# Splitting the last selection group into two pairs and giving score tiles a third PSUM buffer

## Chip, cores and metric

One core of one Trainium2 chip. The metric is the device time of one execution in microseconds (us); several runs are taken and the median is given. TensorE (PE), VectorE (DVE), ScalarE (ACT), GpSimd (POOL) and SyncE (SP, which only issues DMAs here) each work through their own list of instructions in order; semaphores tie the lists together. PSUM, into which TensorE writes, has 8 banks of 512 float32 values for each of 128 partitions, and both kernels use all eight in the stage that is changed.

## What is computed

One layer of a hybrid decoder: a combined projection of x (4096 positions, 1024 features) feeds a sparse attention branch and a state-space branch (S5); both are gated, joined, projected and normalised. The sparse attention first gives every query a score for every earlier key, and keeps the best 256 keys (n_sel is 256, the heads of the scores are 8 of 32):

```python
idx_logits = jnp.einsum('bthd,bsd->bths', qi_b, ki)
index_score = jnp.einsum('bths,bth->bts', jax.nn.relu(idx_logits), wi_b)
index_score = jnp.where(causal[None], index_score, neg)
_, sel = lax.top_k(index_score, n_sel)
c_sel = jax.vmap(lambda cb, ib: cb[ib])(c, sel)
s = jnp.einsum('bthc,btkc->bthk', ql_b, c_sel)
s = jnp.where(valid[:, :, None, :], s, neg)
p = jax.nn.softmax(s, axis=-1)
o = jnp.einsum('bthk,btkc->bthc', p, c_sel)
...
mixed = jnp.concatenate([att * jax.nn.silu(gate_a), ssm * jax.nn.silu(gate_s)], axis=-1)
y = jnp.einsum('bse,ed->bsd', mixed, w_out)
return layer_norm(DEEPNORM_ALPHA * x + y, ln_g, ln_b)
```

All results are float32. The products that need it are made from a high and a low part of each operand in three matmuls (a triple, `mm3`, lines 98 to 100).

## The kernel before

The 4096 positions are 32 tiles of 128 queries. The kernel runs in three stretches: scores, selection and projection together (to about 1790 us), attention with the S5 branch woven into it (to about 3500 us), and the output (to the end).

**The first stretch** has two streams. The projection goes over the positions in eight sweeps of 512 (`prepare` transposes x with TensorE, L483; `sweep` takes 17 columns of the weights and multiplies, 24 matmuls to a column, L98 to L100 on tiles `ps_x`). ScalarE and VectorE empty `ps_x`, and SyncE stores the results. From the second sweep on, POOL loads the split weights from memory (L511), two tiles `w` to a column. The column "kv" makes the keys and values of attention from the latents `c_d` (L513 to L535): eight triples, each emptied by ScalarE (L85) and VectorE (L87) into tiles `st`, of which there are three, and stored to `k_d` (16 stores) and `v_d` (8 stores). The column "ckv" makes the latents, with small sums on TensorE at L574 and L582.

The other stream makes the scores of a query tile (`score`, L238 to L266): TensorE multiplies into `ps_i` (L254, two banks to a tile), ScalarE takes relu of it (L256), VectorE adds it with the head's weight to the row of scores `acc` (L265). Then `select` (L296 to L406) finds the 256th largest score of each row for a group of tiles at a time. It works in up to 8 rounds: count how many scores are above a threshold, move the threshold. The count of one tile goes to VectorE (L329) or ScalarE (L325), by a letter of the pattern in `PAT`; behind the counts stands a chain of small VectorE operations for the whole group (L331 to L367, L346 the one that moves the bounds). After the last round follow final passes over each tile: sign flip on ScalarE (L386), then L390, L391, L393 (the eight largest) and L401 on VectorE, and the mask on ScalarE (L405), which SyncE stores to `mask_d` (L269). A group's rows lie in four `acc` buffers; two groups may be under way.

The list `ORDER` (L147 to L150) says which tiles form a group and in which order groups go: two small groups, two of four tiles, five pairs from 30/31 down to 22/23, and last a group of four, 10, 11, 20 and 21. A group of four counts three tiles on ScalarE and one on VectorE ("AAAD"); a pair alternates one each, one each, both on ScalarE ("DA", "DA", "AA").

A scheduler, which knows the dependencies and places the instructions of the two streams on each engine when the kernel is built, sets the final order; no table is written by hand. It also may move work from one side of the branch that ends the stretch to the other.

**That branch**: L1010 to L1026 add up on VectorE whether any row was lost, TensorE sums it over partitions (L1027), and all engines read the result and jump (L1029, L1030). The code behind the jump (`select_any`) is the fallback for lost rows and does not run with these inputs.

**Attention** then goes pair by pair of query tiles and head by head (`Pair`, L1070 on): scores L1116 and L1117 from `QH`/`QL` and `KT`, mask and maximum on VectorE (L1119), exponential on ScalarE (L1132), transposes (L1149), values (L1161, L1162). SyncE loads the masks (`mb`, L1101), POOL loads keys and values (`KT`, `V`, L1055 and L1057). S5 batches stand between: their matrices are prepared on POOL (L815 to L863) and enter TensorE first at L875.

PSUM in the first stretch: `psi` holds `ps_i` (2 buffers of 2 banks), `pst` holds `ps_x` (4 buffers of 1 bank), eight banks in all.

## Time and profile before

| | us |
|---|---|
| Median of 3 runs | 4118.75 (4113.29 to 4124.88) |
| Profiled execution, its own time | 4111.49 |
| Its span, first to last instruction | 4109.7 |
| TensorE busy (share of the span) | 3683.6 (90%) |
| VectorE busy | 3298.1 (80%) |
| ScalarE busy | 2804.1 (68%) |
| POOL busy | 1545.4 (38%) |
| Mean granted TensorE clock | 0.943 of full |

The profile gives the busy time of an engine over a stretch of the span, the waits (which instruction stood still, for whom, how long in total), the groups of like instructions with the mean length of one, and a timeline. An engine name is followed by tile and line: "DVE acc L265 <- ACT relu L256" is VectorE at line 265, which writes acc, waiting for ScalarE's relu of line 256. Matmuls overlap, so the pitch from one start to the next, not the listed length, is what one costs. All views are of the one profiled execution, whose time stands in the table.

### The profile page before, as it was taken

The page shows a single profiled execution, that of the slowest core. Times are in us where ns is not written, and L with a number is a line of the kernel's source. Part 1 is how long each engine was busy: PE and PEld are TensorE (multiplying, and loading weights), DVE is VectorE, ACT ScalarE, POOL GpSimd, SP SyncE. Part 2 cuts the span into 40 slices and gives each one's busy share as a digit, 9 for nine tenths or more (in the row PEclk, how much of TensorE's full clock was granted, in tenths as well). Part 3 has the DMA queues.
Part 4 walks back from the last instruction along what each step waited for, and adds up shares of the span by engine and source line. Part 5 has one row for each costly group of instructions (what it writes and reads, how often), then busy time and mean ns, then how long its engine had stood idle before and what let it go on. Part 6 is the DMA issues. An engine that isn't in the chain of part 4 may idle for free.

```text
span 4109.7 us, 64216 instructions
## 1 busy us (share of the span) xinstructions
PE 3683.6 (90%) x20925; PEld 3111.3 (76%) x20925; DVE 3298.1 (80%) x6879; ACT 2804.1 (68%) x4540; POOL 1545.4 (38%) x3405
## 2 busy tenths in 40 slices
PE   6788988988989989149999999999999999899998
PEld 5566766766757658038888898888898989788887
DVE  5898898888798888778888888888888889565554
ACT  4587878776767776647777777777777778534342
POOL 1110011111111111236665656666656542354543
PEclk9889989989989899569999999999999999999999
DMA  8766967767668677244545444444444444644441
GB/s 226 159 195 177 307 190 213 200 183 221 190 188 230 185 202 203 71 141 117 154 120 149 124 136 137 128 136 127 140 132 135 119 142 121 181 135 134 143 124 72
DMA packets 521898, 656.19 MB, mean 160 GB/s; under 512 B 126800, under 2 KB 367952, under 8 KB 521552
## 3 DMA queue, kind: packets, MB, share of 16 engines
q1 hardware_dynamic: 438800, 448.54, 37.7%
q0 software_dynamic: 82752, 203.45, 18.5%
q8 instruction: 167, 2.74, 0.3%
q14 instruction: 179, 1.47, 0.1%
HBM read 480.61 MB, written 169.13 MB: 158 GB/s over the span
## 4 chain that ended last, share of the span: by engine, by line
PE 45%; ACT 3%; DMA 3%; issue 2%; DVE 2%; POOL 2%; SPq 0%; ACTq 0%; POOLq 0%; DVEq 0%
PE ps_t L1149 10%; PE ps_o L1161 6%; PE ps_o L1162 5%; PE ps_s L1116 5%; PE ps_s L1117 5%; PE ps_y L99 2%; PE ps_y L98 2%; PE ps_y L100 2%; ACT sc L1132 2%; PE ps L959 2%; PE ps_g L99 1%; PE ps_g L100 1%; PE ps_g L98 1%; DMA mb<-mask_d 1%; ACT ph L85 1%
## 5 line engine op out<-in xcount | busy, mean ns | idle before, releaser
L87 DVE TENSOR_TENSOR pl<-ps_t,ph 128x512 fp32r<-128x512 f32 x1088 | 748.5, 689 | 194.2 <-ACT ph L85 181.1
L85 ACT ACTIVATE ph<-ps_t 128x512 fp32r<-128x512 f32 x1088 | 644.2, 596 | 372.6 <-PE ps_t L1149 353.8
L1119 DVE CUSTOM_DVE_ANT_0 sc<-ps_s,mb 128x512 f32<-128x512 f32 (+3 forms) x1152 | 725.6, 638 | 39.2 <-PE ps_s L1117 18.2
L1161 PE MATMUL ps_o<-ph,V 128*128 128x256 f32 x2176 | 659.3, 325 | 29.9 <-ACT ot L1165 27.0
L1149 PE MATMUL ps_t<-ident,sc 128*128 128x128 f32 x4352 | 655.7, 273 | 10.5 <-DVE pl L87 6.0
L256 ACT ACTIVATE relu<-ps_i 128x1024 f32<-128x1024 f32 (+5 forms) x624 | 534.6, 899 | 168.8 <-PE ps_i L254 147.2
L1132 ACT ACTIVATE sc<-sc,mx 128x1024 f32<-128x1024 f32 (+7 forms) x640 | 637.0, 997 | 7.3 <-DVE mx L1119 7.0
L1149 PEld LDWEIGHTS ps_t<-ident,sc 128*128 128x128 f32 x4352 | 537.0, 141 | 122.6 <-DVE pl L87 6.6
L265 DVE SCALAR_TENSOR_TENSOR acc<-relu,wi,acc 128x2048 f32<-128x2048 f32 (+15 forms) x322 | 558.1, 1733 | 77.2 <-ACT relu L256 74.3
L1162 PE MATMUL ps_o<-pl,V 128*128 128x256 f32 x2176 | 565.0, 282 | 2.6 <-DVE pl L87 2.6
L511 POOL DMA_DIRECT2D w<-w_d x294 | 159.0, 541 | 1085.9 <-PE ps_x L100 1005.8
L98 PE MATMUL ps_x<-xk,w 128*128 128x512 f32 x1280 | 517.1, 404 | 6.5 <-DVE st L87 2.0
L100 PE MATMUL ps_x<-xk,w 128*128 128x512 f32 x1280 | 507.3, 396 | 0.0
L99 PE MATMUL ps_x<-xk,w 128*128 128x512 f32 x1280 | 506.5, 396 | 0.0
L254 PE MATMUL ps_i<-kst,qst 128*128 128x512 f32 (+1 forms) x1136 | 394.9, 446 | 117.2 <-ACT relu L256 111.2
L1116 PE MATMUL ps_s<-KT,QH 128*128 128x512 f32 (+2 forms) x1152 | 438.2, 381 | 19.6 <-DMA V<-v_d 15.2
L1161 PEld LDWEIGHTS ps_o<-ph,V 128*128 128x128 f32 x2176 | 413.5, 190 | 47.4 <-ACT ot L1165 39.5
L1117 PE MATMUL ps_s<-KT,QL 128*128 128x512 f32 (+2 forms) x1152 | 436.4, 379 | 0.7 <-DVE QL L87 0.7
L1162 PEld LDWEIGHTS ps_o<-pl,V 128*128 128x128 f32 x2176 | 417.6, 192 | 7.3 <-DVE pl L87 3.3
L254 PEld LDWEIGHTS ps_i<-kst,qst 128*128 128x128 f32 x1136 | 222.1, 213 | 223.9 <-ACT relu L256 185.7
L325 ACT ACTIVATE junk_a<-acc,s_t 128x1920 int8<-128x1920 f32 (+14 forms) x152 | 333.1, 2191 | 53.8 <-DVE s_t L354 24.1
L98 PEld LDWEIGHTS ps_x<-xk,w 128*128 128x128 f32 x1280 | 245.7, 192 | 70.5 <-DMA w<-w_d 6.2
(408 smaller groups left out, 7435.4 us busy)
## 6 DMA issues: line engine op xcount, KB each, us to landing
w<-w_d POOLq DMA_DIRECT2D x294, 512.0 KB, 4.2
mb<-mask_d SPq DMA_DIRECT2D x416, 256.0 KB, 3.1
xs<-in_x_dram SPq DMA_DIRECT2D x120, 256.0 KB, 4.6
w_d<-w SPq DMA_DIRECT2D x42, 512.0 KB, 4.3
qs_d<-st SPq DMA_DIRECT2D x64, 256.0 KB, 3.0
k_d<-st SPq DMA_DIRECT2D x128, 128.0 KB, 2.4
v_d<-st SPq DMA_DIRECT2D x64, 256.0 KB, 3.5
QL<-qT_d SPq DMA_DIRECT2D x64, 256.0 KB, 4.2
```

The lines of the kernel that those rows point to most:

```text
L85: ACT.activation(hi, src, AF.Copy, scale=scale)
L87: DVE.tensor_tensor(lo, src, ft(hi), op=OP.subtract)
L98: PE.matmul(ps, lh, rh, start=first, stop=False)
L99: PE.matmul(ps, lh, rl, start=False, stop=False)
L100: PE.matmul(ps, ll, rh, start=False, stop=last)
L1116: PE.matmul(ps[:, :nn], QH[:, qs], kk, start=True, stop=False)
L1117: PE.matmul(ps[:, :nn], QL[:, qs], kk, start=False, stop=True)
L1119: DVE.tensor_tensor_reduce(self.sc[a][-1][:, o], ps[:, :n], self.mb[a][:, o], 1.0, TOP, OP.add, OP.min, mx[:, k:k + 1])
L1132: ACT.activation(v, v, AF.Exp, scale=-1.0, bias=nm, accum_out=self.ds[:, a, r:r + 1])
L1149: PE.transpose(pt[:, e, a, :], self.sc[a][r][:, o:o + P], ident)
L1161: PE.matmul(self.po, v, ph_[:, e, :], start=(b + e == 0), stop=False)
L1162: PE.matmul(self.po, v, pl_[:, e, :], start=False, stop=(b + e == self.nb - 1))
```

## The change

The last group of four becomes two pairs, 20/21 and then 10/11. For these two groups `counters` always takes the first entry of the pattern, "DA": the first tile counted on VectorE, the second on ScalarE, in every round. `ps_i` gets a third buffer (6 banks), `ps_x` keeps two (2 banks). There is one group more, so one sum more at L1024; nothing else is edited.

```diff
-    ORDER = SMALL + MIDDLE + LARGE + [[10, 11, 20, 21]]
+    ORDER = SMALL + MIDDLE + LARGE + [[20, 21], [10, 11]]
...
     def counters(group, it):
         p = PAT[len(group)]
-        return p[it % len(p)]
+        return p[0 if group in ORDER[-2:] else it % len(p)]
...
-    psi = idxs.enter_context(tc.tile_pool(name="i_ps", bufs=2, space=PSUM))
+    psi = idxs.enter_context(tc.tile_pool(name="i_ps", bufs=3, space=PSUM))
...
-        pst = ph.enter_context(tc.tile_pool(name="p_t", bufs=4, space=PSUM))
+        pst = ph.enter_context(tc.tile_pool(name="p_t", bufs=2, space=PSUM))
```

With the buffers the scheduler's order changes on every engine. Three places are shown, each with the engine's list before and then in the changed kernel; a line of "..." leaves rows out.

First VectorE in rounds 4 to 6 of the pair 24/25 (a row of 3200 scores is tile 24's count; L265 is a weighted add of the next pair's scores). Before:

```order
L329 TENSOR_SCALAR mk,s_t<-acc,s_t 128x3200
L331 TENSOR_TENSOR s_t<-s_t,cm 128x2
L332 TENSOR_TENSOR s_t<-s_t,ca 128x2
L333 TENSOR_SCALAR s_b<-s_t 128x2
L334 TENSOR_SCALAR s_b<-s_t 128x2
L265 SCALAR_TENSOR_TENSOR acc<-relu,wi,acc 128x2048
L346 COPY_PREDICATED s_ab<-s_b,s_t 128x8
...
L354 TENSOR_TENSOR s_t<-s_ab,s_e 128x2
L265 SCALAR_TENSOR_TENSOR acc<-relu,wi,acc 128x2048
L331 TENSOR_TENSOR s_t<-s_t,cm 128x2
```

In the change:

```order
L329 TENSOR_SCALAR mk,s_t<-acc,s_t 128x3200
L331 TENSOR_TENSOR s_t<-s_t,cm 128x2
L332 TENSOR_TENSOR s_t<-s_t,ca 128x2
...
L346 COPY_PREDICATED s_ab<-s_b,s_t 128x8
...
L354 TENSOR_TENSOR s_t<-s_ab,s_e 128x2
L331 TENSOR_TENSOR s_t<-s_t,cm 128x2
L332 TENSOR_TENSOR s_t<-s_t,ca 128x2
...
L354 TENSOR_TENSOR s_t<-s_ab,s_e 128x2
L329 TENSOR_SCALAR mk,s_t<-acc,s_t 128x3200
L331 TENSOR_TENSOR s_t<-s_t,cm 128x2
```

What moved: before, weighted adds stand between the counts and the small operations of a round; in the change the rounds from the fourth on follow each other without any, and the adds stand together in the first three rounds of a pair and among the final passes of the pair before it. The sixth round has no count on VectorE in either (between L354 and L331 of the last rows).

Second TensorE around its last score matmul (L254) and up to the loss sum (L1027). Before:

```order
L254 MATMUL ps_i<-kst,qst 128x512
L254 MATMUL ps_i<-kst,qst 128x256
L98 MATMUL ps_x<-w,qh 128x512
L99 MATMUL ps_x<-w,qh 128x512
L100 MATMUL ps_x<-w,ql 128x512
L1027 MATMUL ps_i<-lo_14184,ones 1x11
L1029 TENSOR_LOAD lo_14185
```

In the change:

```order
L254 MATMUL ps_i<-kst,qst 128x512
L483 MATMUL ps_x<-ident,xs 128x128 x8
L98 MATMUL ps_x<-qh,w 128x512
L99 MATMUL ps_x<-ql,w 128x512
L100 MATMUL ps_x<-qh,w 128x512
...
L100 MATMUL ps_x<-xk,w 128x512
L574 MATMUL ps_x<-ones,st 128x1 x4
L582 MATMUL ps_x<-st,ones 128x512
...
L100 MATMUL ps_x<-xk,w 128x512
L1027 MATMUL ps_i<-lo_14309,ones 1x12
L1029 TENSOR_LOAD lo_14310
```

What moved: before, the key/value column of the last sweep (`ps_x<-w,qh`) runs out between the last scores, and nothing but it stands ahead of L1027. In the change the last score comes earlier in the list; behind it stand the key/value column of the sixth sweep (24 matmuls), the latent column of the next (24, with L574 and L582) and 16 columns of 24 projection matmuls, and only then L1027.

Third, TensorE and SyncE just behind the branch (L1030). TensorE before:

```order
L1030 UNCONDITIONAL_BRANCH x2
L1116 MATMUL ps_s<-KT,QH 128x256
L1117 MATMUL ps_s<-KT,QL 128x256
...
L1116 MATMUL ps_s<-KT,QH 128x512
L1117 MATMUL ps_s<-KT,QL 128x512
L1149 MATMUL ps_t<-ident,sc 128x128 x4
L875 MATMUL ps_21346<-ident,M_21278 128x128 x2
```

In the change:

```order
L1030 UNCONDITIONAL_BRANCH x2
L98 MATMUL ps_x<-qh,w 128x512 x2
L99 MATMUL ps_x<-ql,w 128x512
L100 MATMUL ps_x<-qh,w 128x512
...
L100 MATMUL ps_x<-qh,w 128x512
L1116 MATMUL ps_s<-KT,QH 128x256
L1117 MATMUL ps_s<-KT,QL 128x256
...
L98 MATMUL ps_x<-w,qh 128x512
L99 MATMUL ps_x<-w,qh 128x512
L100 MATMUL ps_x<-w,ql 128x512
L875 MATMUL ps_21618<-ident,M_21550 128x128 x2
```

SyncE before:

```order
L1063 DMA QL<-qT_d 64x1024 x4
L1101 DMA mb<-mask_d 128x128
L1101 DMA mb<-mask_d 128x256
L1101 DMA mb<-mask_d 128x384
L1101 DMA mb<-mask_d 128x512
...
L1101 DMA mb<-mask_d 128x256
L1063 DMA QL<-qT_d 64x1024 x2
L1101 DMA mb<-mask_d 128x1024
```

In the change:

```order
L1063 DMA QL<-qT_d 64x1024 x4
L1101 DMA mb<-mask_d 128x128
L525 DMA k_d<-st 64x512 x6
L1101 DMA mb<-mask_d 128x256
...
L525 DMA k_d<-st 64x512 x6
...
L525 DMA k_d<-st 64x512 x4
L535 DMA v_d<-st 128x4x128 x5
L825 DMA pk<-pk_d 128x2x115
L535 DMA v_d<-st 128x4x128
L827 DMA U<-u_d 128x2x512
```

What moved: the key/value column of the last sweep now lies behind the branch. Its 24 matmuls stand between the first score rows of attention and L875, and its 16 stores of keys and 8 of values between SyncE's mask loads, with the loads of the first S5 batches (`pk`, `U`) behind and between them. On POOL two loads of `V` and the preparation of the S5 matrices, before it in the list of the kernel before, stand behind the branch too.

## Rows read from the trace of the kernel before

**Rows 1.** Busy us of PE, PEld, DVE, ACT, POOL; then granted clock, DMA share, GB/s.
```profile
100.00:1640.00 1540.00, 1359.22 (x5559) 1041.27 (x5560) 1328.34 (x2288) 1135.23 (x1426) 197.99 (x358) 0.92 0.73 203
1640.00:1690.00 50.00, 17.84 (x55) 11.70 (x54) 41.35 (x60) 29.21 (x42) 17.78 (x27) 0.64 0.56 164
1690.00:1790.00 100.00, 0.20 (x2) 0.12 (x2) 73.04 (x198) 53.13 (x55) 3.74 (x7) 0.50 0.07 25
1830.00:3500.00 1670.00, 1635.88 (x11611) 1484.17 (x11610) 1440.68 (x3677) 1279.07 (x2537) 1002.97 (x2670) 1.00 0.47 132
```

**Rows 2.** Waits of VectorE (DVE), 100 to 1640 us: in total, times, longest.
```profile
DVE acc L265 <- ACT relu L256: 82.9, 64, 7.2
DVE s_t L331 <- ACT junk_a L325: 52.8, 25, 6.0
DVE mk L390 <- ACT acc L386: 18.3, 7, 8.2
```

**Rows 3.** The same view of ScalarE, TensorE and POOL's queue, 100 to 1640 us.
```profile
ACT relu L256 <- PE ps_i L254: 136.6, 101, 6.8
PE ps_i L254 <- ACT relu L256: 109.1, 113, 6.1
POOL w L511 <- PE ps_x L100: 951.9, 258, 25.9
```

**Rows 4.** Timeline of the tail: start, length, engine, instruction, [idle before <- releaser].
```profile
1665.89 1.02 DVE L265 SCALAR_TENSOR_TENSOR acc<-relu,wi,acc 128x768 f32<-128x768 f32 x1 [0.59 <-ACT relu L256]
...
1703.00 3.15 DVE L329 TENSOR_SCALAR_CACHE_REDUCE mk<-acc,s_t 128x2816 uint8<-128x2816 f32 x1
...
1706.35 2.54 ACT L325 ACTIVATE junk_a<-acc,s_t 128x2688 int8<-128x2688 f32 x1
...
1709.01 0.16 DVE L331 TENSOR_TENSOR s_t<-s_t,cm 128x4 f32<-128x4 f32 x1 [2.86 <-ACT junk_a L325]
...
1742.83 7.89 ACT L386 ACTIVATE acc<-acc,s_sg 128x1408 f32<-128x1408 f32 x4 [1.46 <-DVE s_sg L379]
...
1783.05 0.19 DVE L1013 TENSOR_TENSOR fl<-fl 128x32 f32<-128x32 f32 x1 [3.31 <-ACT m L405]
...
1787.18 0.20 PE L1027 MATMUL ps_i<-lo,ones 128*1 128x11 f32 x2 [120.18 <-DVE lo L1025]
```

**Rows 5.** Groups of one shape: count, busy us, mean ns, idle before them.
```profile
L265 DVE SCALAR_TENSOR_TENSOR acc<-relu,wi,acc 128x2048 f32<-128x2048 f32 x126 | 295.5, 2345 | 45.0 <-ACT relu L256 44.2
L256 ACT ACTIVATE relu<-ps_i 128x1024 f32<-128x1024 f32 x416 | 418.5, 1035 | 125.4 <-PE ps_i L254 110.1 <-DVE acc L265 4.9 <-DVE s_f L341 3.1
```

**Rows 6.** Timeline, key/value column of the last sweep, TensorE and SyncE's queue.
```profile
1648.08 2.07 PE L98 MATMUL ps_x<-qh,w 128*128 128x512 f32 x4 [2.19 <-ACT qh L85]
...
1652.30 8.07 SPq L525 DMA_DIRECT2D k_d<-st  x9
...
1666.37 0.63 PE L100 MATMUL ps_x<-w,ql 128*128 128x512 f32 x1
...
1671.00 20.24 SPq L535 DMA_DIRECT2D v_d<-st  x7
```

**Rows 7.** Timeline, four projection matmuls at the two levels of the clock.
```profile
1641.43 0.39 PE L98 MATMUL ps_x<-xk,w 128*128 128x512 f32 x1
...
1641.88 0.39 PE L100 MATMUL ps_x<-xk,w 128*128 128x512 f32 x1
...
1651.01 0.63 PE L100 MATMUL ps_x<-qh,w 128*128 128x512 f32 x1
1651.44 0.63 PE L99 MATMUL ps_x<-ql,w 128*128 128x512 f32 x1
```

**Rows 8.** Timeline behind the branch: POOL, TensorE.
```profile
1793.02 0.20 POOL L1097 MEMSET sc<- 128x128 f32 x1 [50.09 <-DVEq L1030]
...
1802.55 0.58 PE L1116 MATMUL ps_s<-KT,QH 128*128 128x256 f32 x1 [15.17 <-DMA V<-v_d]
...
1814.45 0.64 PE L875 MATMUL ps<-ident,M 128*128 128x128 f32 x2
```

## The prediction

> **What bounds the kernel now.** I read the busy time by stage first. From 100 to 1640 us VectorE works 1328.3 us of 1540 and TensorE, whose matmuls overlap in this count, 1359.1, ScalarE 1135.2; between 1690 and 1790 us TensorE does 0.20 us; from 1830 us on, in attention, it is busy 1635.88 of 1670 us [rows 1]. So attention is TensorE's, whatever comes earlier only shifts it, and the change can act on two things: when the stage of scores, selection and projection ends, and how fast attention starts behind it.
>
> The waits say what holds that stage. VectorE is idle for 211.7 us of the 1540, and most of that has three names: the weighted add L265 waits for relu (82.9), the first small operation of a round, L331, for a count on ScalarE (52.8), and L390 for the sign flip (18.3) [rows 2]. ScalarE in turn waits 136.6 us for score matmuls, and these wait 109.1 us for a score buffer that relu has not yet emptied: with two buffers both complaints stand side by side [rows 3]. Weight loads are no limit, since POOL's queue mostly waits for matmuls to give a weight buffer back [rows 3]. Then comes a tail in which only selection works: TensorE waits 120.18 us for the sum of losses at L1025 [rows 4]. In it a round of the last group has three counts in a row on ScalarE: from 1703.00, when the counts start, to 1709.01, of which VectorE, which has one, waits 2.86 us [rows 4]. Eleven small operations some 0.2 us apart make the round 8.2. The last weighted add starts at 1665.89, the final passes of the four tiles run from 1742.83 to 1783.05, and the loss matmul L1027 is at 1787.18 [rows 4].
>
> **Part 1: where the last score ends.** The order of VectorE's instructions in the change has the weighted adds of a pair gathered together, and rounds 4 to 8 of the pair before without adds between them. The work itself is the same. A 2048 wide add takes 2.345 us and needs two relus of 1.035 us, 2.07 us on ScalarE [rows 5]: gathered, VectorE is the slower of the two and should run nearly without a break once a third score buffer lets ScalarE and TensorE go ahead. Against that, rounds without adds leave VectorE idle where both counts of a pair are on ScalarE, so I keep the 52.8 us of waits at L331 as they are. Of L265's 82.9 I let 28 remain: the first groups, and some 4 us for each of five large pairs. That gives 55 us, and the last add at about 1667 - 55 = 1612. The gain is nothing if the third buffer is not what is missing, and 82.9 + 18.3 = 101 us if all of both waits goes. I take a value near the middle, because part of the relu waits are ScalarE busy with counts and evictions, which no buffer removes.
>
> First what the rows show: the same short gaps come back over hundreds of score groups, 109.1 us on TensorE and 136.6 on ScalarE [rows 3]. The Trainium skill (Perfetto Trace Analysis, Optimization Strategy) says that a gap which repeats on the engine that should be saturated can mean that PSUM is too small to give the next tile a place; taken alone it would give the 101 us. The sum goes by 55 all the same, since the saturated engine is VectorE and its largest gap is of another kind.
>
> **Part 2: the tail.** Splitting the last group gives each engine one count per round. After the last add the order has six rounds of 20/21 and its final passes, then seven rounds of 10/11 and theirs. A round of 20/21 is a VectorE count of 2688 elements (a 2816 wide one takes 3.15 us [rows 4]) and the chain of small operations, some 2.4 us: 5.6, six of them 34. One of 10/11, with half the width, is 4.3: seven are 30. The final passes of the same four tiles took from 1742.83 to 1783.05, 40 us [rows 4], and the losses 4 more: 108 us, against 120 now. But in the change TensorE no longer waits there. Behind its last score stand a whole key/value column (24 matmuls with its evictions; it ran from 1648.08 to 1666.4 for 24 matmuls while scores went between [rows 6], so I take 22), a latent column with its small sums (13), and 16 columns of 24 matmuls. Their pitch at full clock is 0.225 us (two of them from 1641.43 to 1641.88) [rows 7]: 5.4 a column, some 88 in all, and 3 for loads that come late. That is 126 us, more than the 108 of selection, so **TensorE ends the stage**. L1027 then comes at 1612 + 126 = 1738, 49 us before its 1787.18. The bounds on the tail are 108 (columns quicker than selection) and 203: at the lower clock the pitch is 0.43 us (1651.01 to 1651.44) [rows 7], 165 us for the columns instead of 88.
>
> **Part 3: the hand-off.** In the change the key/value column of the last sweep lies behind the branch. The rows of before: POOL resumes at 1793.02, the first attention matmul starts at 1802.55, L875, which makes the matrices of the first S5 batch, at 1814.45 [rows 8]. TensorE's queue is in order, so everything behind L875 waits for it. Now it must come after 24 key/value matmuls and two banks of evictions; SyncE must issue 16 stores of keys and 8 of values between mask loads, and only behind them the loads of the batch; POOL's last two value loads wait for the value stores, and stand ahead of the operations that make L875's operand. The nearest rows: nine key stores took SyncE 8.07 us, seven value stores 20.24, since three staging buffers have to land first [rows 6]. So 16 x 0.9 = 14 and 8 x 2.9 = 23, 37 us until the last value store, then a load and the POOL preparation, some 15: L875 at 52 us after POOL resumes instead of 21.4. That is **30 us later**. The lower bound is the bare matmul time, 24 x 0.225 = 5.4; the upper is the 42 us from 1648.08 to the last value store at 1691.2 with nothing hidden [rows 6].
>
> **The sum**: -49 + 30 = -19 us. The profiled execution took 4111.49, so 4092.5; the median of the three runs, 4118.75, is 7.3 above that execution, so **4100** on the scale of the median. No change can be told from a change of under 0.3%, 12.4 us: faster means under 4106.4, slower over 4131.1. The time of attention itself (rows 1, last) I leave alone: same work, same order, TensorE full.
>
> **Rivals.**
> *A, the buffer is all that was missing.* All 101 us of the waits for relu and sign flip go. The last add is at 1566, L1027 at 1692, 95 us early; with 30 for the hand-off 4054. For it: the 109.1 and 136.6 us stand face to face [rows 3]. Against it: ScalarE also has 1135 us of work in 1540 [rows 1].
> *B, the hand-off is cheap.* Stores and evictions hide behind the loads for which attention waits anyway until 1802.55 [rows 8]; only some 6 us remain: -49 + 6, 4076. Against it: the chain through the value stores is serial.
> *C, the gains and the hand-off cancel.* Some 35 us instead of 55 at the last add: -29 + 30, 4119.
> *D, slower: the last add does not move.* VectorE is within 14% of full already, and two single banks instead of four make transposes, projection columns and latent columns wait for each eviction, so that what the third buffer gives the scores is taken back by the projections on the same engines. Then the last add stays near 1667, the tail is 126 instead of 120 (+6) and the hand-off costs 30: 4155. It decides as soon as the last add gains less than 24 us. For it: in before, projections are done early under four banks, and the order of the change shows 144 triples of them left at the last score where before had nearly none.
> *E, slower: the tail runs on the lower clock.* Between 1640 and 1690 us, where TensorE had gaps between key/value groups, the granted clock was 0.64 in the mean [rows 1] and matmuls at its lower level, 1.2 GHz, took the 0.43 pitch [rows 7]. If the columns of the new tail, passing two banks in turn, do so too, the tail grows by 77: -19 + 77, 4177. The Trainium skill (TensorE: Matmul & The Clock Gate, "A second HAM failure mode: psum-queue depth-cycling") speaks for this: a kernel that cycles through PSUM banks had short idle gaps between matmul groups, and its clock went back and forth. The trace is against it as far as it goes: before, columns that alternated banks held 0.92 of full clock over the whole stage [rows 1].
>
> **How the numbers follow.** The forecast has 0.36 (a quarter of it ends within 12 us of no change), A 0.10, B 0.15, C 0.16, D 0.17, E 0.06. Faster: 0.27 + 0.10 + 0.15 = 0.52. Same: 0.09 + 0.16 = 0.25. Slower: 0.23. The likeliest case's own range is 4080 to 4112. The range 4050 to 4150 takes in B, C, most of A and the lower part of D, and leaves out E, more than half of D and the far end of A, some 0.18.
>
> **What would show it.** Right: waits of L265 for relu down by about half; last add near 1612; TensorE busy after it without a break at full clock until L1027 near 1738, which then waits little or not for L1025; L875 some 50 us behind POOL's resumption, with value stores and POOL's value loads in the chain. Wrong: the last add still near 1667 (D), or TensorE waiting at L1027 for L1025 by more than 10 us (then selection ends the stage, and the tail is mine to have missized); L875 within 30 us (B); granted clock well under full between the last score and L1027 (E).

## The result, and the profile after

The changed kernel takes 4183.22 us (median of 5 runs, 4181.74 to 4184.33) against 4118.75 for the kernel before: a ratio of 1.0161, with a 95% interval of 1.0147 to 1.0175. It is slower by 64 us, where 19 us less was forecast, and lies above the range of 4050 to 4150. Its profiled execution took 4181.74 us with a span of 4179.8, 70.1 us more than before. Of runs 8, 10 and 12 below one execution each came at a far lower granted clock (0.80, 0.55 and 0.29 of full) and took far longer; it is left out of their times and ratios.

Busy time by stretch in the changed kernel (columns as in [rows 1]):

```profile
100.00:1640.00 1540.00, 1285.06 (x5044) 956.19 (x5045) 1306.24 (x2265) 1115.63 (x1380) 179.11 (x316) 0.88 0.65 184
1692.00:1824.00 132.00, 108.86 (x435) 83.10 (x435) 105.40 (x334) 63.02 (x75) 20.80 (x38) 0.90 0.76 217
1824.00:1884.00 60.00, 18.59 (x44) 11.17 (x44) 12.75 (x34) 11.89 (x25) 23.74 (x44) 0.54 0.82 232
1890.00:3560.00 1670.00, 1636.97 (x11608) 1484.55 (x11607) 1442.09 (x3686) 1279.75 (x2541) 1012.14 (x2684) 1.00 0.47 133
```

Attention takes what it took: 1636.97 us of TensorE in 1670 (1635.88 in [rows 1]). In the stage before it, up to 1640 us, TensorE has done 1285.06 us instead of 1359.22 and at a lower mean clock, 0.88 instead of 0.92; VectorE has done 22 us less too, so its idle time is 233.8 us instead of 211.7.

The waits of VectorE, ScalarE and TensorE from 100 to 1640 us, to be read beside [rows 2] and [rows 3]:

```profile
DVE s_t L331 <- ACT junk_a L325: 98.0, 31, 13.0
DVE acc L265 <- ACT relu L256: 32.3, 33, 4.0
DVE mk L390 <- ACT acc L386: 23.9, 8, 4.4
DVE xk L87 <- ACT xk L85: 21.0, 15, 4.9
...
ACT relu L256 <- DVE acc L265: 56.4, 46, 9.2
ACT relu L256 <- PE ps_i L254: 54.5, 36, 4.9
...
PE ps_i L254 <- ACT relu L256: 112.8, 123, 8.5
PE ps_x L483 <- DVE xk L87: 54.2, 30, 10.4
PE ps_x L98 <- DVE st L87: 17.0, 19, 2.9
PE ps_x L98 <- DVE xk L87: 14.2, 5, 8.5
```

Four lines of the kernel before that its rows above do not have, from the same three views:

```profile
DVE xk L87 <- ACT xk L85: 6.1, 5, 2.5
...
ACT relu L256 <- DVE acc L265: 8.8, 7, 3.3
...
PE ps_x L98 <- DVE st L87: 19.3, 16, 3.4
PE ps_x L483 <- DVE xk L87: 7.1, 7, 3.7
```

L265 waits 32.3 us for relu instead of 82.9, as was expected of the third buffer. L331 waits 98.0 us for counts instead of 52.8, so the two together have 130.3 us instead of 135.7. ScalarE now stands still for VectorE, because the relu tiles are full (56.4 instead of 8.8). And TensorE has a wait of another kind: transposes (L483) for VectorE to empty a single bank, 54.2 us, where that was 7.1 before. VectorE in turn waits longer for ScalarE's high part of the transposed tiles (`xk`), 21.0 us instead of 6.1; that is the largest rise behind the one of L331.

The timeline of the tail and the hand-off, to be read beside [rows 4] and [rows 8]:

```profile
1690.50 1.82 DVE L265 SCALAR_TENSOR_TENSOR acc<-relu,wi,acc 128x1536 f32<-128x1536 f32 x1
...
1819.70 0.16 DVE L1025 TENSOR_REDUCE lo<-lo 128x1 f32<-128x11 f32 x1
...
1823.50 0.39 PE L100 MATMUL ps_x<-xk,w 128*128 128x512 f32 x1
1823.82 0.20 PE L1027 MATMUL ps_i<-lo,ones 128*1 128x12 f32 x2
...
1829.74 0.20 POOL L1097 MEMSET sc<- 128x128 f32 x1 [7.88 <-DVEq L1030]
...
1859.82 4.88 SPq L535 DMA_DIRECT2D v_d<-st  x5
...
1865.20 0.10 POOL L953 MEMSET V<- 128x4 f32 x1 [12.21 <-PE ps_x L100]
1867.41 0.61 POOL L856 TENSOR_TENSOR RM<-ident,pk 128x256 f32<-128x256 f32 x1 [2.10 <-DMA pk<-pk_d]
...
1871.71 1.89 POOL L815 TENSOR_TENSOR Uh<-U,zeros 128x1024 fp32r<-128x1024 f32 x1 [2.94 <-DMA U<-u_d]
1873.54 1.16 POOL L1057 DMA_DIRECT2D V<-v_d  x2
...
1883.02 0.68 POOL L846 TENSOR_TENSOR M<-M,tmp 128x256 f32<-128x256 f32 x1
...
1883.75 0.69 PE L875 MATMUL ps<-ident,M 128*128 128x128 f32 x2 [18.61 <-POOL M L846]
```

| | before | after | |
|---|---|---|---|
| last weighted add ends | 1666.9 | 1692.3 | +25.4 |
| from there to L1027 | 120.3 | 131.5 | +11.2 |
| from L1027 to L875 | 27.3 | 59.9 | +32.6 |
| from L875 to the end of VectorE's last instruction (L1359) | 2291.2 | 2292.4 | +1.2 |

The four rows add up to 70.4 us, against 70.1 between the spans, which end with the last store behind L1359. L1027 follows TensorE's last projection matmul (1823.50) without waiting for L1025, which was through at 1819.86: TensorE ends the stage, as forecast, but selection was through only 4 us earlier.

### The profile page after: what moved, and what is told of

Read it like the earlier page. It is cut to its first block, busy times and chain, and to the rows that moved or that the text cites. A ratio compares the mean times of both kernels' runs of the same rounds, so it can differ in the third digit from the quotient of the medians.

```text
span 4179.8 us, 64540 instructions
## 1 busy us (share of the span) xinstructions
PE 3750.8 (90%) x20925; PEld 3127.8 (75%) x20925; DVE 3314.4 (79%) x7009; ACT 2798.5 (67%) x4524; POOL 1545.7 (37%) x3403
## 4 chain that ended last, share of the span: by engine, by line
PE 44%; ACT 3%; DMA 3%; POOL 2%; issue 2%; DVE 2%; SPq 0%; ACTq 0%; POOLq 0%; DVEq 0%
PE ps_t L1149 9%; PE ps_o L1161 5%; PE ps_o L1162 5%; PE ps_s L1116 5%; PE ps_s L1117 5%; PE ps_y L99 2%; PE ps_y L100 2%; PE ps_y L98 2%; ACT sc L1132 2%; PE ps L959 2%; PE ps_g L98 1%; PE ps_g L99 1%; PE ps_g L100 1%; ACT ph L85 1%; POOL tmp L940 1%
## 5 line engine op out<-in xcount | busy, mean ns | idle before, releaser
L265 DVE SCALAR_TENSOR_TENSOR acc<-relu,wi,acc 128x2048 f32<-128x2048 f32 (+15 forms) x322 | 560.9, 1743 | 40.8 <-ACT relu L256 37.6
L98 PE MATMUL ps_x<-xk,w 128*128 128x512 f32 x1280 | 521.7, 408 | 32.6 <-DMA w<-w_d 8.4
L254 PE MATMUL ps_i<-kst,qst 128*128 128x512 f32 (+1 forms) x1136 | 404.5, 460 | 125.2 <-ACT relu L256 116.4
L254 PEld LDWEIGHTS ps_i<-kst,qst 128*128 128x128 f32 x1136 | 224.3, 220 | 239.1 <-ACT relu L256 200.8
L325 ACT ACTIVATE junk_a<-acc,s_t 128x1920 int8<-128x1920 f32 (+15 forms) x144 | 322.3, 2238 | 45.9 <-DVE s_t L354 28.5
L98 PEld LDWEIGHTS ps_x<-xk,w 128*128 128x128 f32 x1280 | 246.9, 193 | 108.5 <-issue 18.5
```

The lines of the kernel that those rows point to most:

```text
L98: PE.matmul(ps, lh, rh, start=first, stop=False)
```

## The experiments

Each run stands against runs of the kernel before on the same chip (medians from 4107 to 4112 us; the change against the 4118.75 above); the ratio with its 95% interval is what compares them. In the profiles of all runs of this table the stretch from L875 (its start) to the end of L1359 lasts 2286 to 2296 us, so each difference arises before L875. Single runs of the kernel before spread over as much as 18 us on one chip (4103.19 to 4121.23), so a difference of some 10 us between single profiles is a hint and no more. An edit also changes the order that the scheduler gives: what a run shows is the edit together with the order that comes with it.

| run | what it has | ratio (95% interval) | last add ends | L1025 ends | L875 starts |
|---|---|---|---|---|---|
| before | | 1 | 1666.9 | 1787.0 | 1814.5 |
| the change | split, 3 double + 2 single | 1.0161 (1.0147 to 1.0175) | 1692.3 | 1819.9 | 1883.7 |
| 1 | split alone | 1.0068 (1.0048 to 1.0088) | 1693.6 | 1816.3 | 1844.4 |
| 2 | 3 double + 2 single alone | 1.0231 (1.0214 to 1.0248) | 1635.0 | 1801.3 | 1908.7 |
| 3 | the change, old counters | 1.0205 (1.0188 to 1.0222) | 1705.3 | 1845.4 | 1900.0 |
| 4 | the change, one count each in all pairs | 1.0197 (1.0180 to 1.0214) | 1678.8 | 1805.9 | 1897.5 |
| 5 | 2 double + 2 single | 1.0233 (1.0217 to 1.0249) | 1666.4 | 1794.9 | 1904.7 |
| 6 | 2 double + 3 single | 1.0078 (1.0062 to 1.0093) | 1687.3 | 1808.0 | 1834.4 |
| 7 | before, last four counted two and two | 1.0010 (1.0001 to 1.0019) | 1677.6 | 1786.0 | 1812.2 |
| 8 | split alone, old counters | 1.0053 (1.0033 to 1.0074) | 1674.0 | 1800.6 | 1829.3 |
| 9 | split alone, 10/11 counted on ScalarE | 1.0047 (1.0030 to 1.0064) | 1667.0 | 1791.0 | 1819.5 |
| 10 | before, score tiles of one bank | 1.0037 (1.0020 to 1.0053) | 1674.1 | 1796.9 | 1824.0 |

### The two parts alone

Run 1 is the change with the two PSUM lines undone:

```diff
-    psi = idxs.enter_context(tc.tile_pool(name="i_ps", bufs=3, space=PSUM))
+    psi = idxs.enter_context(tc.tile_pool(name="i_ps", bufs=2, space=PSUM))
...
-        pst = ph.enter_context(tc.tile_pool(name="p_t", bufs=2, space=PSUM))
+        pst = ph.enter_context(tc.tile_pool(name="p_t", bufs=4, space=PSUM))
```

> Only the split of the last group and its fixed counters; PSUM as before (two score buffers, four single banks). Theory 1 (PSUM is what costs): waits of VectorE at L331 for counts between 100 us and the last weighted add stay near the 53 us of before (98 in the change), waits at L265 near 83 to 87, last weighted add within 10 us of 1667, projections done before it, TensorE idle in the tail, L875 some 21 us behind POOL's resumption; the tail is selection alone, 108 us against 120, so the time is 4105 to 4120. Theory 2 (the split is what costs, since it makes two groups' rounds run without adds between them): waits at L331 near 98, last add after 1685, time 4150 or more.

Neither theory got it right: 1.0068, with the waits of theory 1 and the late last add of theory 2 (27 us), at a time (4142.54 us) between the two. VectorE's waits in run 1 from 100 to 1640 us, then TensorE's in the tail:

```profile
DVE acc L265 <- ACT relu L256: 91.8, 68, 7.3
DVE s_t L331 <- ACT junk_a L325: 49.5, 26, 5.9
```

```profile
PE ps_i L1027 <- DVE lo L1025: 133.1, 1, 133.1
```

The waits are those of before, so no round was stripped of adds. The busy time of all engines up to L1025 tells what is longer, in the kernel before and in run 1:

```profile
100.00:1787.00 1687.00, 1377.06 (x5613) 1052.98 (x5613) 1442.54 (x2544) 1217.57 (x1520) 219.51 (x392) 0.89 0.68 191
```

```profile
100.00:1816.00 1716.00, 1384.65 (x5615) 1057.13 (x5615) 1470.38 (x2673) 1207.15 (x1504) 230.65 (x394) 0.88 0.67 188
```

VectorE (third of the five busy times) has 1470.38 us of work instead of 1442.54, 27.8 more, and its idle time is the same (1716 - 1470.4 = 245.6 against 1687 - 1442.5 = 244.5). The split gives 16 rounds where there were 8: eight more chains of small operations, and on VectorE eight counts of tile 10 beside those of the wide tile. The stage ends 29.3 us later. The prediction had only shortened the tail by sums of rounds, and the tail itself is as long as before (122.8 against 120.3). In the change VectorE's work up to L1025 is only 14.0 us above the kernel before, and its idle time 19.0 us above:

```profile
100.00:1820.00 1720.00, 1432.31 (x5640) 1066.56 (x5641) 1456.58 (x2667) 1211.58 (x1503) 204.34 (x364) 0.89 0.66 186
```

Run 2 is the other half: the kernel before with these two lines as in the change.

> Only the PSUM layout: three double score buffers, two single banks; groups as before. Theory 1: the waits go as in the change: L331 near 98 or more, L265 near 35 to 40, transposes L483 behind VectorE's xk near 54, last add 1675 to 1700, projections and the key/value column left for the tail and behind the branch, L875 over 50 us behind POOL's resumption, time 4165 to 4200. Theory 2: near 4119, L331 near 53.

1.0231, 4207.19 us: the PSUM layout alone costs more than the whole change, a little over theory 1's 4200. The last add is 32 us earlier, as Part 1 of the prediction wanted in kind and neither theory had it, but some 160 projection triples and a key/value column are left for the tail, and a key/value column with 44 triples for the time behind the branch, so L875 comes at 1908.7. Both parts harm, the layout by 2.3% and the split by 0.7%; together (1.6%) they cost less than the layout alone. The traces show where: in run 2 L1027 stands at 1810.4 and L875 98.3 us behind it, in the change at 1823.8 and 59.9 us; the later stage end of the change has the 44 triples before the branch, beside selection, instead of behind it. How much of that interplay is the order of the list and how much the chip, no run separates.

### Third score buffer or two single banks

Run 5 takes only single banks away from the kernel before, run 6 one of them:

```diff
-        pst = ph.enter_context(tc.tile_pool(name="p_t", bufs=4, space=PSUM))
+        pst = ph.enter_context(tc.tile_pool(name="p_t", bufs=2, space=PSUM))
```

> The kernel before with two single banks instead of four and nothing in their place: score buffers stay at two double ones, two banks of PSUM idle. Theory 1 (the two single banks cost, the third score buffer gives a little back): transposes L483 wait 45 us or more for xk, projections are left for the tail and behind the branch, and the time is that of the run with the whole PSUM layout (4207) or up to 25 us above it. Rival (the third score buffer is what harms, since it lets the scheduler gather the adds and strips rounds of them): waits at L331 stay near 53, L265 near 87, and the time is under 4150.

> The kernel before with three single banks, two double score buffers, one bank idle. Theory 1: a part of the loss, growing with what is left for the tail: 25 projection triples and a key/value column stand between the last score and the loss sum, which the selection tail of 120 us covers, and nothing stands behind the branch; so 4112 to 4135, L875 under 30 us behind L1027. Rival: within 0.3% of 4112.

1.0233 with two (4204.67 us, theory 1; the rival's 4150 is out) and 1.0078 with three (a little above the expected end, 4137.28 us). Run 5 has one score buffer less than run 2 and the same time. The waits from 100 to 1640 us of VectorE and TensorE, in run 2 and then in run 5:

```profile
DVE s_t L331 <- ACT junk_a L325: 82.0, 25, 10.5
DVE acc L265 <- ACT relu L256: 56.2, 44, 6.3
...
PE ps_i L254 <- ACT relu L256: 114.5, 123, 8.5
PE ps_x L483 <- DVE xk L87: 48.9, 31, 5.2
PE ps_x L98 <- DVE st L87: 36.4, 19, 9.5
```

```profile
DVE acc L265 <- ACT relu L256: 78.8, 50, 5.3
DVE s_t L331 <- ACT junk_a L325: 63.8, 27, 8.5
...
PE ps_i L254 <- ACT relu L256: 124.8, 151, 3.9
PE ps_x L483 <- DVE xk L87: 44.2, 30, 7.7
PE ps_x L98 <- DVE st L87: 13.1, 21, 1.3
```

In run 2 VectorE waits 56.2 us for relu and 82.0 for counts, in run 5 78.8 and 63.8: 138 us and 143. **The third buffer changes the name of the wait, not its sum.** And the transposes' wait is there in both (48.9 and 44.2). So the loss belongs to the two single banks, and the third buffer is worth nothing beside them. What it does is to bring the last add forward, from 1666.4 (run 5) to 1635.0 (run 2); L1025 comes 6 us later all the same, so the end of the adds does not tell when the stage ends.

Run 10 asks after the number of score buffers in the kernel before without touching the single banks: four score tiles of one bank in place of two of two banks, relu on 512 elements. The scores have four banks as before, and ScalarE has more to do (busy 1244.22 us up to L1025 instead of 1217.57).

```diff
-    psi = idxs.enter_context(tc.tile_pool(name="i_ps", bufs=2, space=PSUM))
+    psi = idxs.enter_context(tc.tile_pool(name="i_ps", bufs=4, space=PSUM))
...
-                for q0 in range(0, n, 2 * C):
-                    m = min(2 * C, n - q0)
-                    pi = psi.tile([P, 2 * C], FT, name="ps_i")
+                for q0 in range(0, n, C):
+                    m = min(C, n - q0)
+                    pi = psi.tile([P, C], FT, name="ps_i")
```

> The kernel before with score tiles of one bank, four of them instead of two of two banks, and relu on 512 elements at a time; single banks stay four. If the number of score buffers is what holds the stage (rival A of the prediction), waits of L254 for relu and of L265 fall by half and the time is under 4095. If buffers are not what is missing, ScalarE's added 0.15 us for each 1024 elements (some 60 us of work) makes it 4120 to 4160, with waits at L265 for relu as long as before or longer.

1.0037 (4123.4 us). The waits, VectorE and TensorE, 100 to 1640 us:

```profile
DVE acc L265 <- ACT relu L256: 76.9, 62, 4.5
DVE s_t L331 <- ACT junk_a L325: 67.5, 27, 6.8
...
PE ps_i L254 <- ACT relu L256: 84.9, 76, 7.1
```

TensorE's wait for relu falls from 109.1 us to 84.9 and VectorE's from 82.9 to 76.9, but L331 has 67.5 instead of 52.8. More and smaller buffers give nothing, with waits at L265 some 6 us shorter where they were expected as long as before; as they add no bank, it is runs 2 and 5 that speak against rival A, the buffer as all that was missing, and run 10 only supports them.

### Who stands still for want of a single bank

Run 11 is the change, but ScalarE also copies the transposed tile out of PSUM, so that VectorE subtracts outside it:

```diff
-                split(xk[:, 0], xk[:, 1], ps.rearrange("p a t -> p (a t)"))
+                ACT.activation(xk[:, 0], ps.rearrange("p a t -> p (a t)"), AF.Copy)
+                ACT.activation(xs, ps, AF.Copy)
+                DVE.tensor_tensor(xk[:, 1], xs.rearrange("p a t -> p (a t)"), ft(xk[:, 0]), op=OP.subtract)
```

> The change, whose transposed tiles of x leave PSUM by two ScalarE passes (high part, and a plain copy into the tile that was transposed); VectorE then subtracts from that copy, outside PSUM. The work of VectorE is the same, ScalarE has some 64 passes of 0.6 us more (38 us). If TensorE falls behind in the change because VectorE, far back in its queue, holds one of only two single banks (theory M), the 55 us that transposes (L483) and the 16 that columns (L98) wait for VectorE's xk fall to under 25 together, fewer projections are left behind the last score, and the time falls from 4183 to 4130 to 4170. If the bank count matters in another way (ScalarE's queue holds the banks as long, or the stage is VectorE's work alone), it stays within 10 us of 4183 or rises by up to 40.

4183.07 us, ratio 1.0180 (1.0163 to 1.0197): no gain. TensorE's waits, 100 to 1640 us:

```profile
PE ps_x L98 <- DVE st L87: 38.5, 19, 9.5
PE ps_x L483 <- DMA xs<-in_x_dram: 34.6, 15, 7.7
PE ps_x L483 <- ACT xs L486: 27.4, 38, 2.0
```

The transposes no longer wait for VectorE, but 34.6 us for the loads of x, whose tiles the edit keeps longer, and 27.4 for ScalarE. The edit moved the wait; it did not test the bank.

Three more kernels divide the single banks instead. Each is the kernel before with a pool of its own for transposes: run 13 has two banks for columns and one for transposes, run 14 (its edit is shown) two and two, run 15 one and two.

```diff
-        pst = ph.enter_context(tc.tile_pool(name="p_t", bufs=4, space=PSUM))
+        pst = ph.enter_context(tc.tile_pool(name="p_t", bufs=2, space=PSUM))
+        psr = ph.enter_context(tc.tile_pool(name="p_r", bufs=2, space=PSUM))
...
-                ps = pst.tile([P, 4, P], FT, name="ps_x")
+                ps = psr.tile([P, 4, P], FT, name="ps_r")
```

> The kernel before with two double score buffers, two single banks for projection columns and what follows them, and one bank for transposes alone (seven banks). With three banks shared it was 4137, with two shared 4204 (before 4107 to 4112). If transposes are what stands still for want of a bank, and take the columns' bank while they do (theory T), a bank of their own is worth as much as a third shared one: 4120 to 4145, with waits at L98 as in before. If columns and their small followers need more than two banks (theory C), the time is 4180 to 4215 and TensorE's waits at L98, L546, L574 and L582 stay as with two shared banks.

> The same with two banks for transposes (eight banks, as in before, but divided). Theory T: 4105 to 4125. Theory C: 4170 to 4215, since the columns have two banks as in the change.

> One single bank for columns, two for transposes (seven banks). Theory T: a column of 5.4 us waits for the eviction before it, some 2 us with the queues, at 136 columns 270 us of which a part is covered by scores: above 4200 all the same, and below 4300. Theory C: above 4300.

| single banks | ratio (95% interval) | loss sum ready (L1025) | S5 begins (L875) | triples between L1027 and L875 |
|---|---|---|---|---|
| 4 shared (before) | 1 | 1787.0 | 1814.5 | 0 |
| 2 + 2 divided (run 14) | 1.0049 (1.0033 to 1.0066) | 1809.7 | 1837.7 | 0 |
| 3 shared (run 6) | 1.0078 (1.0062 to 1.0093) | 1808.0 | 1834.4 | 0 |
| 2 + 1 divided (run 13) | 1.0117 (1.0093 to 1.0142) | 1783.5 | 1848.6 | 8 |
| 2 shared (run 5) | 1.0233 (1.0217 to 1.0249) | 1794.9 | 1904.7 | 64 |
| 1 + 2 divided (run 15) | 1.0713 (1.0687 to 1.0738) | 1744.2 | 2101.3 | 293 |

(Lines of the kernel before; in runs 13 to 15 they are one higher. The triples are those of the projection and of the key/value column, counted in the traces.)

Runs 13 and 14 (4154.98 and 4130.55 us) lie above theory T's ranges, but nearer to them than to theory C's. Run 15 (4402.66 us) is above theory T's 4300, where theory C had it. So neither theory holds alone. With two banks for columns in all three cases, two banks of their own for transposes take the loss from 2.33% to 0.49%, one takes it to 1.17%. TensorE's waits of run 13 and of run 14, 100 to 1640 us (`ps_r` are the transposes):

```profile
PE ps_r L484 <- DVE xk L87: 41.1, 22, 6.5
PE ps_x L98 <- DVE st L87: 24.4, 14, 5.7
PE ps_x L98 <- ACT xk L85: 12.1, 6, 5.0
```

```profile
PE ps_r L484 <- DVE xk L87: 19.9, 16, 3.8
...
PE ps_x L98 <- DVE st L87: 7.9, 8, 2.5
```

Transposes wait 41.1 us with one bank and 19.9 with two, and columns (L98) less as well. So most of the loss, some 1.8 of 2.3%, comes from transposes and columns having only two banks between them. That it is the transposes' own wait is not shown: run 13 has nearly that of run 5 (41.1 and 44.2) at half the loss.

The table shows where the time goes, and it is another place than the waits: in run 5 selection is through only 7.9 us later than before, and 82 of the 90 us by which L875 is late lie behind that, as TensorE has projections left to do behind the branch, where selection no longer runs beside them. In runs 6 and 14 it is the other way round: nothing is left behind the branch, and selection ends later. How run 5 gets there can be followed in TensorE's list: up to 600 us it has done 425 score matmuls and 277 triples, the kernel before 409 and 389; up to 1600 us 1119 and 1084 against 1108 and 1282. The first 155 or so instructions of that list are those of before, and the last of them starts 7.7 us later (69.3 us against 61.6), with 3.6 us of waits of transposes for `xk` instead of 0.6: a part of the delay needs no other order on TensorE. From there on the lists differ. How much of the loss is waits for a bank, and how much the order that the scheduler makes for fewer banks, no run separates: a kernel with two banks and the order of before was not run.

### Counters

Run 3 undoes the fixed counters in the change, runs 8 and 9 vary them in the split alone, run 4 takes `PAT[2]` as `("DA",)`, run 7 gives the undivided last group the pattern "DAAD" (the edits in this order: runs 3 and 8, run 9, run 4, run 7):

```diff
-        return p[0 if group in ORDER[-2:] else it % len(p)]
+        return p[it % len(p)]
...
-        return p[0 if group in ORDER[-2:] else it % len(p)]
+        return "AA" if group is ORDER[-1] else p[0 if group in ORDER[-2:] else it % len(p)]
...
-    PAT = {2: ("DA", "DA", "AA"), 3: ("ADA",), 4: ("AAAD",), 5: ("ADADA",)}
+    PAT = {2: ("DA",), 3: ("ADA",), 4: ("AAAD",), 5: ("ADADA",)}
...
-        p = PAT[len(group)]
+        p = ("DAAD",) if group is ORDER[-1] else PAT[len(group)]
```

> The change without its fixed counters for the last two groups (their third and sixth rounds count both tiles on ScalarE again). Theory 1: selection ends some 4 us later at most, and TensorE ends the stage anyway, so the time is that of the change within 10 us (4175 to 4195), with half of the key/value column back before the branch. Theory 2 has no other number here.

1.0205 (4196.8 us): a little slower than expected, with half of the key/value column back before the branch as expected. Selection ended at 1845.4 and L1027 stood at 1845.5, so here selection ended the stage, not TensorE.

> The change with one count on each engine in every round of every pair. If the added waits at L331 are rounds in which both counts of a pair are on ScalarE and VectorE has nothing between (theory 1a), they fall from 98 to under 50, VectorE's busy time grows by some 3.5 us for each of ten such rounds, and the last add comes 10 to 30 us earlier: 4150 to 4175. If the waits come from the gathering of adds whichever engine counts (theory 1b), L331 stays near 90 and the time is within 10 us of 4183 or later.

VectorE's waits of run 4, 100 to 1640 us:

```profile
DVE s_t L331 <- ACT junk_a L325: 44.9, 18, 7.4
DVE acc L265 <- ACT relu L256: 37.0, 28, 4.4
```

The wait at L331 is halved, as theory 1a has it, and the last add is 13.5 us earlier. The time is not: 4192.15 us. L1025 comes 14 us earlier than in the change and L1027 11 us (1812.4), but 24 more triples are left behind the branch, and L875 comes 13.8 us later. Taking that wait away buys nothing here.

> The kernel before, whose last group of four counts the first and last tile (10 and 21) on VectorE and the middle two on ScalarE, in every round. If the tail's round is set by three counts in a row on ScalarE (theory 1), it falls from some 8.2 to 7.0 us, eight rounds give 8 to 10 us, and as all eight rounds lie behind the last weighted add the added VectorE work is covered by its waits of 2.86 us: the stage ends 5 to 10 us earlier, 4102 to 4108. If something else sets it, the time is within 4 us of 4112.

1.0010, no gain. The tail got shorter by 11.7 us (to 108.6; 8 to 10 were expected), but the last add came 10.7 us later. The scheduler's list for VectorE differs from that of before from about 80 us on, so whether the lost time is the order or the 10.7 us of added VectorE work (1453.20 up to L1025 against 1442.54) stays open.

> The split of the last group alone, with the old alternation of counters (third and sixth round of each pair on ScalarE) and PSUM as before. In the split with fixed counters the stage ended 29 us later with VectorE's work up to L1025 28 us higher and its idle time unchanged. If it is VectorE's work that counts wherever it lies (theory W), four counts fewer on VectorE (two of 2688, two of 1408, some 9 us) give 4130 to 4136 on the scale on which the fixed split had 4142.5 and before 4112.5. If it is the chain of rounds behind the last add that counts (theory L), four rounds become 2 to 3 us longer each, and the time is 4145 to 4155.

> As the split alone, but both tiles of 10/11 are counted on ScalarE in every round. Theory W: eight counts of 1408 elements fewer on VectorE, 13 us of work: 4125 to 4133 on the same scale. Theory L: each of the eight rounds behind the last add grows from some 4 to 5.6 us: 4150 to 4158.

4129.5 and 4126.3 us; with their ratios and the 4112.5 of the expectation's scale, 4134 and 4132, both where theory W put them. Theory L's 4145 to 4158 is excluded. VectorE's work up to L1025 (the same view as for run 1) is 1458.17 and 1452.88 us instead of 1470.38, and L1025 comes at 1800.6 and 1791.0 instead of 1816.3, although single rounds behind the last add are longer. That the two runs are faster than run 1 is not certain: the intervals of the ratios overlap, and 16 and 25 us between single profiles are not far from their spread. And theory W does not hold wherever work is added: in run 7 VectorE has 10.7 us more work than before and L1025 comes 1 us earlier, in run 4 33 us more than in the change (1489.98 against 1456.58) and L1025 comes 14 us earlier; idle time shrank instead.

### Less work for VectorE in the kernel before

Run 12 is the edit of run 11 in the kernel before, with the subtraction on POOL.

> The kernel before with the same two ScalarE passes, the subtraction on POOL: 64 subtractions of 0.68 us, 44 us, leave VectorE. If the stage of before ends by VectorE's work wherever it lies (theory W), up to 44 us go: 4065 to 4095. If the stage's end is as much ScalarE's (38 us more work there, 1135 of 1540 us busy) and POOL's queue holds the low parts back behind its weight loads, the time is 4100 to 4140.

4194.05 us, 1.0211 (1.0191 to 1.0232), worse than either side of the expectation. POOL's subtractions waited 61.9 us for ScalarE's copies in a queue that also issues weight and query loads, transposes waited 37.9 for loads of x, columns 51.3 for VectorE, and L265 111.7 for relu (all to 1690 us). Nor did VectorE lose work, as the run had meant it to: a subtraction takes POOL 1.62 us where it took VectorE 0.68, and VectorE's other instructions became longer at the same number (L265 647.0 us in all instead of 627.7, L390 57.5 instead of 44.8), so that VectorE was busy 1466.40 us up to the loss sum instead of 1442.54. Why they became longer is not shown. So the run does not test theory W.

No run was faster than the kernel before.

## Why the prediction was wrong

**Part 2 and Part 3 were right in size.** From the last add to L1027 126 us were forecast and 131.5 measured, ended by TensorE as said. The tail of selection beside it was not right: 108 us were forecast, and L1025 ended 127.5 us behind the last add, so it was close to ending the stage itself. TensorE's granted clock was 0.53 to 0.83 up to 1740 us, while the key/value and the latent column came with gaps, and 1.00 from there to the end of the tail; most of the 136 projection triples ran at the 0.23 us pitch. So rival E had the time nearly (4177), but its mechanism, a tail longer by 77 us, did not occur. L875 was put 52 us behind POOL's resumption and came after 54.0. Its inside was different: five value stores took 4.88 us, 1 us each and not 2.9, but the key stores before them, spread between mask loads, ended only 30 us behind POOL's resumption instead of 14. What held POOL was first the key/value matmuls (12.21 us at L953, until 1865.20), then the loads (2.10 and 2.94 us) and some 13 us of its own preparation. There the sum was right by errors that cancel, which is luck.

**The step that failed is Part 1**: "I keep the 52.8 us of waits at L331 as they are", and with it "The work itself is the same". The sum turned 55 us less waiting at L265 into a last add 55 us earlier, and put the loss of two single banks at nothing. The last add came 25.4 us later. Selection's end came 33 us later (14.0 us more work on VectorE, 19.0 us more idle time), L1027 another 4 us behind it, and the hand-off took 32.6 us more, near the 30 of the sum. Three things stand in the place of that step.
- Waits were treated as separate sums. L265 fell by 50.6 us in the same stretch (55 were forecast), but L331 rose by 45.2; VectorE's whole idle time did not fall but rose by 22 us. Runs 2 and 5 show that this pair trades at a nearly constant sum and the time does not follow it.
- The two single banks were costed at nothing in the forecast, and appear only in rival D. They are the main cost: 2.3% alone (run 5), and 1.8 of it gone when transposes have two banks of their own (run 14). The sum had no term for it: before, transposes waited only 7.1 us, with four banks to pass through, and a price for two was never bounded. How the loss comes about, by waits on the chip or by the order, stays open.
- The split was credited with its shorter rounds, and not charged with the eight more chains and counts on VectorE, 28 us, which come out in full in run 1, where the split stands alone.

Rival D (the last add does not move, 4155) was the nearest in mechanism: two single banks take back what the third buffer gives. It had 0.17, and stopped at "does not move".

**Rivals A, B and C** are out: A by runs 2 and 5, supported by run 10; B because the hand-off cost 32.6 us; C because no gain was left to cancel.

## What to carry to other kernels

When buffers of one kind are traded for another, price the one that is taken: ask for each user of the smaller pool how long it holds a bank, and through how many busy engines it has to go before it is free. A wait that shrinks is a gain only if the waits around it stay; look at an engine's work and total idle time up to the point that matters, not at one row of its waits. Splitting a group costs its fixed operations once more: run 1 paid nearly all of their 27.8 us. And where a scheduler lays out the lists, look first at which work it has moved to the other side of a branch or a stage's end: in run 5 most of the loss stands there, and none of the waits up to 1640 us names it.

## What had not been expected of the hardware

One bank fewer at the narrow end costs far more than the named waits add up to: with a single column bank (run 15) the kernel lost 293 us, 7.1%, though columns waited for the evictions of columns only 27.7 + 21.9 + 19.1 = 69 us up to 1650 us. In the same profile TensorE waited 196.8 us for relu, 87 more than in the kernel before up to 1650 us (109.8), though the score buffers were the same. The time itself is lost in one place: the loss sum L1028 (L1027 before) stands at 1744.3, 43 us earlier than before, but L876 (L875 before) at 2101.3, 357 us behind it, and in between TensorE does 272 projection triples and 21 of the key/value columns, at a granted clock of 0.82. So it is two sweeps' columns that lie behind the branch. How the bank leads to that, through waits on the chip or through the order of the list, no run separates.
